# Ten gate tiles in pairs of seven half-block products, with the block sums kept in the place of the input's fp32 copy

## The chip, the cores and the metric

One core of a Trainium2 chip runs the whole layer as one program. The metric is the device time of one execution in microseconds (us); the kernel before has a median of 1524.26 us over three runs (1524.18 to 1525.2). Engines are named as in the profile: PE (TensorE matmul), PEld (its weight load), DVE (VectorE), ACT (ScalarE), POOL (GpSimd), SP (SyncE, which here only issues DMAs).

## The reference, cut to what matters

One layer: modulated attention of two branches (A windowed, B global), merged by sigmoid gates, then a ConvFFN. What this change touches is the modulated input `h`, the projection of the gates, and the query of branch B:

```
mod = silu(c) @ w_mod + b_mod                     # 6 vectors of 1024
h = x * (1 + scale1) + shift1                     # 1024 tokens x 1024
proj = h @ w_in + b_in                            # q_a, k_a, v_a, q_b, k_b, v_b, gates (2048 columns)
q_b = rope(qk_rms(proj[q_b columns]))
g_a, g_b = split(sigmoid(proj[gate columns]))     # 2 x 1024 channels
y = (g_a * (o_a @ w_branch_a) + g_b * (o_b @ w_branch_b)) @ w_out
```

The mod vectors `scale1` and `shift1` are needed before `h`; the other four and two for the context tokens are computed later, beside the projections.

## The kernel before, in words

All matmuls are in fp32 precision by parts: each operand is split into a high part `hi` (written as fp32r) and a low part `lo = x - hi`; `split` (L80) makes both, `mm3` (L89) issues hi·hi, hi·lo and lo·hi into one accumulation. So one 128x128 weight tile against 512 tokens is three matmul instructions, and each weight tile of 128x512 needs one split: `hi` on ACT (L82) and `lo` on DVE or POOL (L87).

**Stage 1 (L200 to L306).** `h` is kept transposed: eight tiles of 128 channels by 1024 tokens. For each of them SP loads x (`xr`, L218) and two tiles of `w_mod`, DVE computes shift and scale as dot products (`mod`, L193, one instruction of 128x1024), ACT writes `hh` (L241) and, in place, the fp32 `h` (L242), DVE writes `hl` (L245). PE meanwhile accumulates the eight token tiles of q_b in the eight banks of PSUM (L303 to L306). At its end DVE writes the eight q_b tiles to SBUF (`q_evac`, L378).

**The projections (L816 to L868).** An `order` list, built from `GORD` (L46, L805), interleaves 16 gate tiles with four groups: qa and qb (w_qa against four token tiles each) and ka and kb (w_kv against five each). A gate tile (`gate`, L769) is 128 channels by 1024 tokens: for each half of 512 tokens, eight channel tiles times three matmuls, 48 in all; then a sigmoid on ACT (L783) and a store to DRAM on ACT's queue (L784). With `GORD = 3, 4, 4, 1, 4` the order is 3 gates, qa, 4 gates, qb, 4 gates, ka, 1 gate, kb, 4 gates. Weights come through a ring of `RAWB` raw tiles (`fetch_raw`, L699) and are split ahead of their use (`prefetch`, L716) into a ring of eight split tiles (`wsplit`, L160). A gate's `lo` parts are on POOL (L722), those of the four groups on DVE.

Beside these, after each block of matmuls, run the remaining 48 mod vectors: `mods` (L755) spreads them by a span of PE time, each a 512 KB load by SP into a ring of `WRING` tiles (L751) and one DVE instruction. `side_step` (L794) takes one step at a time of the work on finished projections: rms and rotary of q_b (`qpost`, L383), rotary of q_a, and the keys (`kv_post`, L423).

**Order on the queues.** Up to the start of the ka group all five engines are under `manual_schedule` (L269, closed at L822): each engine executes its instructions in the order in which the program traces them, SP's DMAs too. After it a scheduler orders them. A waiting instruction holds up everything behind it on its engine.

**Memory.** `hp` is a pool of 19 slots of 128x1024 fp32 (L129), handed out and given back by name (`ht`, `hput`). In stage 1 the x tiles and `w_mod` tiles are temporary in it (`tmp`, L187).

## Time and profile before

| | us |
|---|---|
| median of three runs | 1524.26 |
| the profiled execution, its own time | 1523.1 |
| its span, first to last instruction | 1521.3 |
| PE busy in the span | 1503.2 (99%) |
| DVE / ACT / POOL busy in the span | 1168.3 / 786.1 / 751.3 |
| first and last matmul of a gate start at | 56.2 and 332.2 |

The profiled execution shows 1.8 us around its span, and it is 1.2 us below the median of the runs. A timeline row gives start, duration, engine, line, operation and tiles, and in brackets the idle time before it and what ended that. A row of windows gives the stretch, its length, and busy time (instructions) of PE, PEld, DVE, ACT and POOL, then the granted clock, the DMA share and GB/s. Times in the rows are from the start of the span.

### The profile page before, as it was taken

What the parts mean: (1) busy time and instruction counts of PE and PEld (TensorE: products, weight loads), DVE (VectorE), ACT (ScalarE), POOL (GpSimd) and SP (SyncE); (2) the same over time, 40 slices, a digit from 0 to 9 for tenths busy, and PEclk for the clock granted to TensorE, in tenths of its full rate; (3) what the DMA queues carried; (4) which work ended last, traced back from release to release, by engine and by line L of the source; (5) the groups of instructions that cost most, each with busy time, mean ns of one, the idle gap of its engine ahead of it and who ended that gap; (6) DMA issues with size and microseconds to landing.
All of it is one profiled execution on the core that took longest, in us unless ns stands there. A gap on an engine that the chain in (4) does not pass through costs nothing.

```text
span 1521.3 us, 22183 instructions
## 1 busy us (share of the span) xinstructions
PE 1503.2 (99%) x7812; PEld 1263.3 (83%) x7812; DVE 1168.3 (77%) x1751; ACT 786.1 (52%) x1303; POOL 751.3 (49%) x727
## 2 busy tenths in 40 slices
PE   8999999999999999999999999999999999999997
PEld 7888888888988888887888998888888888888887
DVE  6667986539988787877865788888888888557884
ACT  5322222439988677667234555444444444435552
POOL 0356532426776677766124346666666773111121
PEclk9999999999999999999999999999999999999998
DMA  9777672322234576653541322333344448996731
GB/s 370 266 242 242 223 252 87 106 82 68 67 108 104 131 172 167 153 121 89 207 160 42 104 77 98 111 111 111 111 111 111 112 111 238 340 271 210 255 105 56
DMA packets 114399, 232.09 MB, mean 153 GB/s; under 512 B 13200, under 2 KB 28048, under 8 KB 114192
## 3 DMA queue, kind: packets, MB, share of 16 engines
q1 hardware_dynamic: 99056, 201.82, 39.8%
q0 software_dynamic: 10400, 20.19, 8.8%
q10 hardware_dynamic: 4832, 8.68, 1.5%
q8 instruction: 61, 1.00, 0.3%
q14 instruction: 50, 0.41, 0.1%
HBM read 179.45 MB, written 65.86 MB: 161 GB/s over the span
## 4 chain that ended last, share of the span: by engine, by line
PE 92%; DVE 3%; ACT 2%; issue 1%; DMA 1%; POOL 1%; SPq 0%; DVEq 0%; ACTq 0%; POOLq 0%
PE ptr L604 5%; PE p L90 4%; PE p L91 4%; PE p L92 4%; PE g L90 4%; PE g L92 4%; PE g L91 4%; PE av L627 4%; PE av L628 3%; PE b L90 3%; PE b L92 3%; PE b L91 3%; PE s L496 3%; PE s L497 3%; PE c L90 2%; PE c L92 2%
## 5 line engine op out<-in xcount | busy, mean ns | idle before, releaser
L616 DVE TENSOR_TENSOR ptl<-ptr,pth 128x512 fp32r<-128x512 f32 x195 | 128.2, 685 | 20.2 <-ACT pth L615 18.0
L547 ACT ACTIVATE p<-p,nm 128x1280 f32<-128x1280 f32 (+2 forms) x128 | 139.8, 1093 | 6.6 <-DVE p L545 5.9
L87 DVE TENSOR_TENSOR ld<-rd,hd 128x1024 fp32r<-128x1024 f32 x77 | 94.8, 1250 | 50.5 <-ACT hd L82 48.3
L615 ACT CAST pth<-ptr 128x512 fp32r<-128x512 f32 x195 | 111.3, 590 | 30.3 <-PE ptr L604 28.7
L82 ACT CAST hd<-rd 128x1024 fp32r<-128x1024 f32 x77 | 79.3, 1048 | 82.2 <-PE p L92 55.7
L604 PEld LDWEIGHTS ptr<-identr,pb 128*128 128x128 f32 x944 | 96.3, 140 | 23.7 <-ACT pb L550 3.0
L604 PE MATMUL ptr<-identr,pb 128*128 128x128 f32 x944 | 107.5, 245 | 1.5 <-ACT pb L550 1.0
L87 POOL TENSOR_TENSOR wlg<-wg,whg 128x512 fp32r<-128x512 f32 x32 | 48.6, 1529 | 121.7 <-ACT whg L82 80.8
L627 PE MATMUL av<-pth,VT 128*128 128x512 f32 x236 | 104.2, 441 | 0.5 <-ACT side L639 0.3
L90 PE MATMUL p<-hd 128*128 128x512 f32 x264 | 103.2, 391 | 0.0
L92 PE MATMUL p<-hd,ld 128*128 128x512 f32 x264 | 102.8, 389 | 0.0
L91 PE MATMUL p<-ld,hd 128*128 128x512 f32 x264 | 102.7, 389 | 0.0
L90 PE MATMUL g<-hh,whg 128*128 128x512 f32 x256 | 99.9, 390 | 0.0
L92 PE MATMUL g<-hh,wlg 128*128 128x512 f32 x256 | 99.7, 389 | 0.0
L91 PE MATMUL g<-hl,whg 128*128 128x512 f32 x256 | 99.6, 389 | 0.0
L628 PE MATMUL av<-ptl,VT 128*128 128x512 f32 x236 | 97.5, 413 | 0.3 <-DVE ptl L616 0.2
L545 DVE TENSOR_SCALAR_CACHE_REDUCE p<-s,cvt,nmc 128x1024 f32<-128x1024 f32 x64 | 84.2, 1317 | 5.2 <-PE s L497 5.2
L496 PE MATMUL s<-KL,q 128*128 128x512 f32 (+2 forms) x192 | 73.6, 384 | 1.3 <-DVE p L545 0.8
L497 PE MATMUL s<-KL,q 128*128 128x512 f32 (+2 forms) x192 | 71.8, 374 | 0.0
L783 ACT ACTIVATE sg<-g,bgc 128x512 f32<-128x512 f32 x32 | 22.0, 686 | 96.2 <-PE g L92 91.4
L82 ACT CAST wS<-s 128x512 fp32r<-128x512 f32 x76 | 45.3, 620 | 48.7 <-POOL s L1236 47.9
L82 ACT CAST wA<-ru 128x512 fp32r<-128x512 f32 x57 | 35.5, 623 | 62.6 <-PE d L92 33.6
(434 smaller groups left out, 4866.9 us busy)
## 6 DMA issues: line engine op xcount, KB each, us to landing
wml<-in_wmodT_dram SPq DMA_DIRECT2D x48, 512.0 KB
ru<-in_w_up_dram SPq DMA_DIRECT2D x38, 512.0 KB
rd<-td SPq DMA_DIRECT2D x55, 256.0 KB
rd<-sd SPq DMA_DIRECT2D x44, 256.0 KB
rd<-in_w_dn_dram SPq DMA_DIRECT2D x33, 256.0 KB
wm<-in_wmodT_dram SPq DMA_DIRECT2D x16, 512.0 KB
wg<-in_w_g_dram SPq DMA_DIRECT2D x32, 256.0 KB
sgd<-sg ACTq DMA_DIRECT2D x32, 256.0 KB
```

The lines of the kernel that those rows point to most:

```text
L82: nc.scalar.copy(hi, src)
L87: lo_eng.tensor_tensor(out=lo, in0=src, in1=hi.bitcast(F32), op=ALU.subtract)
L90: nc.tensor.matmul(ps, a[0], b[0], start=start, stop=False, skip_group_check=resumed)
L91: nc.tensor.matmul(ps, a[0], b[1], start=False, stop=False, skip_group_check=resumed)
L92: nc.tensor.matmul(ps, a[1], b[0], start=False, stop=stop, skip_group_check=resumed)
L496: nc.tensor.matmul(o, self.q[0][:, hs], ks, start=True, stop=False)
L497: nc.tensor.matmul(o, self.q[1][:, hs], ks, start=False, stop=stop)
L547: nc.scalar.activation(row, row, AF.Exp, bias=self.nm[:, hs], scale=-1.0, accum_out=self.sm[:, hs])
L604: i = nc.tensor.transpose(tr[:, h * P:(h + 1) * P], self.bits[:, h, n * P:(n + 1) * P], identr)
L616: nc.vector.tensor_tensor(out=lo, in0=tr, in1=hi.bitcast(F32), op=ALU.subtract)
L627: nc.tensor.matmul(self.av, v, hi, start=first, stop=False)
L628: nc.tensor.matmul(self.av, v, lo, start=False, stop=self.left == 0)
```

## The change

Gates 2 to 11 are computed in five pairs. For a pair the weights are seen as 2x2 blocks A11, A12, A21, A22 (two gate tiles by two halves of the 1024 channels) and `h` as blocks B11, B12, B21, B22 (two halves of the channels by two halves of the tokens). The product of 2x2 blocks is formed from seven block products instead of eight (`spair`): A11·B11, S2·T2, S1·T1, S3·T3, A12·B21, S4·B22, A22·T4, with four sums of weight blocks S1 to S4 (`ssum`, POOL) and four sums of input blocks T1 to T4. A product is 4 channel tiles times 3 matmuls (`sprod`); the results are combined on DVE, ACT and POOL, and each of the four half tiles goes through the sigmoid and to DRAM (`gout`).

The input sums are made once (`hbuild`), in place of the fp32 copies `xr`, which now keep their slots through stage 1 instead of being temporary, and are split into tiles of their own. To have room, the q_b tiles go from PSUM through a small buffer to DRAM (`qd`) and are read back after the last pair; rope tables are loaded then too, and the q_b work (`qpost(1, t)`) is queued from there. The pool has 20 slots, the ring of mod weights 3 tiles instead of 4, the raw ring 4 instead of 3, the `pw` buffers 6 instead of 5, and the scratch of GpSimd's DMAs is 4096 instead of 8192. The order is now gates 0 and 1, the five pairs, qa, qb, ka, kb, gates 12 to 15. Every second `lo` of the qa and qb weights moves from DVE to POOL, and `side_step` always takes one new item.

```diff
-GORD = 3, 4, 4, 1, 4
-PWB = 5
+GORD = 0, 0, 0, 0, 4
+NPAIR = 5
+PWB = 6
...
-RAWB = 3
+RAWB = 4
...
-WRING = 4
+WRING = 3
...
+    qd = [dpool.tile([P, 2, HALF], F32, tag=f"qd{n}", name=f"qd{n}") for n in range(NT // 2)]
...
-    hfree = [(hp, f"H{n}") for n in range(19)]
+    hfree = [(hp, f"H{n}") for n in range(20)]
...
-    ropet = ht("ropet", (P, 2, NT, HD))
-    ropec, ropes = ropet[:, 0], ropet[:, 1]
...
-        x = tmp(f"xr{k}")
+        x = ht(f"xr{k}")
...
-        nc.sync.dma_start(ropec, rope_c)
-        nc.sync.dma_start(ropes, rope_s)
...
-    sqq = [ht("sqq", (P, 2, 512))]
...
-        q_evac(1, t, acc[t], bias_qb)
+        q = pw(f"qb{t}")
+        nc.vector.tensor_tensor(out=q, in0=acc[t], in1=bias_qb, op=ALU.add)
+        nc.sync.dma_start(qd[t // 2][:, t % 2], q)
+    hB = {}
+    def hbuild(k):
+        (b11, b12), (b21, b22) = [[st1[f][1][:, hf * HALF:(hf + 1) * HALF] for hf in (0, 1)] for f in (k, k + 4)]
+        def sub(e, o, a, b):
+            e.tensor_tensor(out=o, in0=a, in1=b, op=ALU.subtract)
+        def parts(n, src, e):
+            if k == 3 and n != "A22":
+                t = [qp.tile([P, HALF], R32, tag={"S1": "q1", "S2": "q2", "S3": "qs"}[n], name=f"T{n}{a}", bufs=2)
+                     for a in "hl"]
+            else:
+                t = ht(f"T{n}_{k}", (P, 2, HALF), R32)
+                t = [t[:, 0], t[:, 1]]
+            split(src, *t, nc.scalar, e)
+            hB[n, k] = t
+        sub(nc.vector, b11, b12, b11)
+        sub(nc.gpsimd, b12, b22, b12)
+        sub(nc.vector, b22, b22, b11)
+        parts("S1", b11, nc.vector)
+        sub(nc.gpsimd, b21, b21, b22)
+        parts("S2", b22, nc.vector)
+        parts("S3", b12, nc.gpsimd)
+        parts("A22", b21, nc.vector)
+        hput(f"xr{k}", f"xr{k + 4}")
...
+    sraw, sw = {}, {}
...
+            if gi == "s":
+                f = 2 * k + 2
+                sraw[k, f"A1{a + 1}"] = r = raw(f"ws{k}_{a}")
+                nc.sync.dma_start(r.rearrange("p (a b) -> p a b", b=P), w_g[f][:, 4 * a:4 * a + 4])
+                for b in (0, 1) if a == 0 else ():
+                    sraw[k, f"A2{b + 1}"] = r = pw(f"wt{k}_{b}")
+                    nc.sync.dma_start(r.rearrange("p (a b) -> p a b", b=P), w_g[f + 1][:, 4 * b:4 * b + 4])
+                continue
...
+        if gi == "s":
+            return
...
-        w, c = wsplit(wr, f"{nm}{k}"), None
+        w, c = wsplit(wr, f"{nm}{k}", "gpsimd" if gi > 1 and k % 2 else "vector"), None
...
-    wring, sring = ([hfree.pop(0) for _ in range(n)] for n in (WRING, 2))
...
-    queue = [qpost(1, t) for t in range(NT)]
-    gates = list(range(2 * KT))
+    queue = []
+    gates = [0, 1] + list(range(2 + 2 * NPAIR, 2 * KT))
+    def ssum(j, n):
+        def sub(o, a, b, op=ALU.subtract):
+            nc.gpsimd.tensor_tensor(out=o, in0=a, in1=b, op=op)
+        if n == "S1":
+            sraw[j, "S1"] = e = pw(f"we{j}")
+            sub(e, sraw[j, "A21"], sraw[j, "A22"], ALU.add)
+        elif n == "S3":
+            sraw[j, "S3"] = r = sraw.pop((j, "A21"))
+            sub(r, sraw[j, "A11"], r)
+        elif n == "S2":
+            sraw[j, "S2"] = r = sraw.pop((j, "A11"))
+            sub(r, sraw[j, "S1"], r)
+        else:
+            sraw[j, "S4"] = r = sraw.pop((j, "A12"))
+            sub(r, r, sraw.pop((j, "S2")))
+            raws[1] += 2
+    SLE = {"A11": "gpsimd", "S2": "vector", "S1": "gpsimd", "S3": "vector", "A12": "gpsimd", "S4": "vector",
+           "A22": "vector"}
+    def ssplit(j, n):
+        sw[j, n] = wsplit(sraw[j, n], f"s{n}_{j}", SLE[n])
+    HB = {"A11": (0, 0), "A12": (4, 0), "S4": (4, 1)}
+    def sprod(j, n, o, start):
+        h, l = sw.pop((j, n))
+        for k in range(4):
+            c = slice(k * P, (k + 1) * P)
+            if n in HB:
+                f, hf = HB[n]
+                b = [x[:, hf * HALF:(hf + 1) * HALF] for x in hT[k + f]]
+            else:
+                b = hB[n, k]
+            mm3(o, (h[:, c], l[:, c]), b, start and k == 0, k == 3, not start)
+        mods(12)
+    def sfirst(j):
+        ssum(j, "S1")
+        ssum(j, "S3")
+        ssplit(j, "A11")
+        ssum(j, "S2")
+        for n in ("S2", "S1", "S3"):
+            ssplit(j, n)
+    def gout(o, src, f, hf):
+        nc.scalar.activation(o, src, AF.Sigmoid, bias=bgc[:, f:f + 1])
+        nc.scalar.dma_start(sgd[f][:, hf * HALF:(hf + 1) * HALF], o)
+    def spair(j, more):
+        f = 2 * j + 2
+        a, b, c, d = (acc_tile(f"s{n}{j}") for n in "abcd")
+        pe, ve = (ph1.tile([P, 512], F32, tag="kv", name=f"{n}{j}", bufs=KVB) for n in ("pe", "ve"))
+        y = [p.tile([P, 2, HALF], F32, tag=t, name=f"y{n}_{j}", bufs=1) for n, (p, t) in enumerate(sring)]
+        y11, y12, y21, y22 = y[0][:, 0], y[0][:, 1], y[1][:, 0], y[1][:, 1]
+        def add(e, o, p, q):
+            e.tensor_tensor(out=o, in0=p, in1=q, op=ALU.add)
+        sprod(j, "A11", a, True)
+        nc.scalar.copy(pe, a)
+        ssplit(j, "A12")
+        sprod(j, "S2", b, True)
+        add(nc.vector, ve, b, pe)
+        ssum(j, "S4")
+        ssplit(j, "S4")
+        fetch_raw()
+        if more:
+            ssum(j + 1, "S1")
+            ssum(j + 1, "S3")
+        sprod(j, "S1", c, True)
+        nc.scalar.copy(y22, c)
+        ssplit(j, "A22")
+        sprod(j, "S3", d, True)
+        add(nc.vector, y22, d, y22)
+        add(nc.gpsimd, y22, y22, ve)
+        if more:
+            ssplit(j + 1, "A11")
+            ssum(j + 1, "S2")
+        else:
+            pf()
+        sprod(j, "A12", a, False)
+        gout(y11, a, f, 0)
+        gout(y22, y22, f + 1, 1)
+        if more:
+            ssplit(j + 1, "S2")
+        else:
+            pf()
+        sprod(j, "S4", c, False)
+        add(nc.vector, y12, c, ve)
+        if more:
+            ssplit(j + 1, "S1")
+        else:
+            pf()
+        gout(y12, y12, f, 1)
+        sprod(j, "A22", d, False)
+        add(nc.vector, y21, d, ve)
+        if more:
+            ssplit(j + 1, "S3")
+        else:
+            pf()
+        gout(y21, y21, f + 1, 0)
+        if not more:
+            hput(*[f"T{n}_{k}" for k in range(4) for n in ("S1", "S2", "S3", "A22") if k < 3 or n == "A22"])
...
-        n = 0 if slow[0] and turn[0] % 2 else 1
+        n = 1
...
-    order = []
+    order = [("g", gates.pop(0)) for _ in (0, 1)] + [("s", j) for j in range(NPAIR)]
...
-    rawq += [(gi, k, a) for gi, k in order for a in ((0, 1) if gi == "g" else (0,))]
+    rawq += [(gi, k, a) for gi, k in order for a in ((0, 1) if gi in ("g", "s") else (0,))]
...
-    for _ in range(WRING // 2):
-        fetch()
...
-    ahead = [2 if gi in (0, 2, 3) else 4 for gi, _ in order]
-    span[1] = sum(6 * KT if gi == "g" else 1.5 * len(groups[gi][2])
+    ahead = [2 if gi in (0, 2, 3) else 8 if gi == "s" else 4 for gi, _ in order]
+    span[1] = sum(6 * KT if gi == "g" else 84 if gi == "s" else 1.5 * len(groups[gi][2])
...
-    nxt = 0
+    nxt = [0]
+    def pf():
+        prefetch(*order[nxt[0]])
+        nxt[0] += 1
+    pf()
+    pf()
+    wring = [hfree.pop(0) for _ in (0, 1)]
+    for k in range(4):
+        hbuild(k)
+    wring.append(hfree.pop(0))
+    sring = [hfree.pop(0) for _ in (0, 1)]
+    for _ in range(2):
+        fetch()
...
-        while nxt < len(order) and sum(ahead[n:nxt + 1]) <= 8:
-            prefetch(*order[nxt])
-            nxt += 1
+        while nxt[0] < len(order) and sum(ahead[n:nxt[0] + 1]) <= 8:
+            pf()
+        if gi == "s":
+            spair(k, k + 1 < NPAIR)
+            if k + 1 == NPAIR:
+                ropet = ht("ropet", (P, 2, NT, HD))
+                ropec, ropes = ropet[:, 0], ropet[:, 1]
+                nc.sync.dma_start(ropec, rope_c)
+                nc.sync.dma_start(ropes, rope_s)
+                sqq = [ht("sqq", (P, 2, 512))]
+                for t in range(0, NT, 2):
+                    Q[1, t] = ht(f"Q1_{t}", (P, 2, 512))
+                    nc.sync.dma_start(Q[1, t], qd[t // 2])
+                queue += [qpost(1, t) for t in range(NT)]
+            continue
...
+                    if order[n + 1:n + 2] == [("s", 0)]:
+                        sfirst(0)
...
-    nc = _bacc.Bacc("TRN2", target_bir_lowering=False, num_devices=1, dynamic_dma_scratch_size=8192)
+    nc = _bacc.Bacc("TRN2", target_bir_lowering=False, num_devices=1, dynamic_dma_scratch_size=4096)
```

In the diff `sraw` holds raw weight tiles, `sw` their split parts, `sring` two slots for the four half tiles of a pair; `pe` and `ve` are intermediate sums, and `b11` to `b22` are the four halves of two `xr` tiles.

## The prediction

> **What bounds the kernel now.** I read the page first, then the projections by windows, then the engines' timelines around the first gate, where the change puts its new work.
>
> ```profile
> PE 1503.2 (99%) x7812; PEld 1263.3 (83%) x7812; DVE 1168.3 (77%) x1751; ACT 786.1 (52%) x1303; POOL 751.3 (49%) x727
> ```
> ```profile
> 56.20:90.00 33.80, 33.80 (x150) 27.97 (x149) 22.23 (x38) 9.36 (x14) 10.96 (x14) 1.00 0.73 251
> ...
> 110.00:155.00 45.00, 45.00 (x200) 37.29 (x199) 34.75 (x64) 12.07 (x19) 30.29 (x30) 1.00 0.75 254
> ...
> 175.00:220.00 45.00, 45.00 (x200) 37.28 (x199) 40.27 (x53) 10.84 (x18) 21.76 (x14) 1.00 0.71 250
> ...
> 326.00:345.00 19.00, 17.65 (x116) 15.02 (x114) 9.54 (x29) 12.51 (x33) 4.38 (x9) 1.00 0.22 70
> ```
>
> PE is busy for all of each stretch of projections, at a granted clock of 1.00. So a matmul removed here is worth its full cadence, and a wait of PE that is added here is paid in full: nothing later gives it back, since PE is 99% busy over the span. DVE is the second load: 40.27 of 45 us near 200 us, without holding PE.
>
> **The matmuls removed.** The pace of PE comes from two rows of one gate; between their starts lie 22 steps of three matmuls.
>
> ```profile
> 62.12 0.39 PE L92 MATMUL g<-hh,wlg 128*128 128x512 f32 x1
> ...
> 77.08 0.39 PE L92 MATMUL g<-hh,wlg 128*128 128x512 f32 x1
> ```
>
> 14.96 us for 66 matmuls is 0.2267 us each (the 0.39 us of a row overlaps its neighbours). Ten gates had 10 x 48 = 480; five pairs have 5 x 7 x 12 = 420. 60 x 0.2267 = **13.6 us less** PE work. A gate is 10.9 us, a block product 2.72 us, a pair 19.04 us.
>
> **The start of gate 0.** Today gate 0 starts straight behind the q_b matmuls, because its weights were loaded and split beforehand:
>
> ```profile
> L90 PE MATMUL g<-hh,whg x256: 387/389/466, 56.2 to 331.8; 128*128 128x512 f32 x128
> ```
> ```profile
> 37.11 4.92 SPq L705 DMA_DIRECT2D wg<-in_w_g_dram  x3
> ```
> ```profile
> 49.52 1.65 ACT L82 CAST whg<-wg 128x512 fp32r<-128x512 f32 x3
> ```
> ```profile
> 50.20 3.79 POOL L87 TENSOR_TENSOR wlg<-wg,whg 128x512 fp32r<-128x512 f32 x3 [38.80 <-DMA gcol<-in_qg_dram]
> ```
> ```profile
> 51.67 5.45 DVE L378 TENSOR_TENSOR Q<-q1acc,bias_qb 128x512 f32<-128x512 f32 x8 [1.74 <-PE q1acc L92]
> ```
>
> The change traces eight stores of q_b on SP ahead of `fetch_raw`. SP is under the manual order, so the loads of gate 0, issued at 37 us today, now stand behind a store that waits for the last of the eight DVE evacuations, at 51.67 + 5.45 = 57.1 us. How long a load takes to land I bound by a wait for one:
>
> ```profile
> 127.18 1.33 SPq L751 DMA_DIRECT2D wml<-in_wmodT_dram  x3
> ```
> ```profile
> 131.39 1.28 DVE L193 CUSTOM_DVE_ANT_0 wml<-wml,sc,bmc 128x1024 f32<-128x1024 f32 x1 [1.59 <-DMA wml<-in_wmodT_dram]
> ```
>
> That is at most 4.2 us from the first of three issues (0.44 us each) for 512 KB; the gate's tile is 256 KB, so I take 3.0, with 2 and 4.2 as ends. [...] Then: issue 57.5, landed 60.5, `hi` 0.55 us on ACT to 61.1, `lo` 1.26 us on POOL to 62.4, where the third matmul can go; today that one starts at 56.2 + 0.45 = 56.7. **+5.7 us** (4.7 to 7), and the two gates end at 56.2 + 21.8 + 5.7 = 83.7.
>
> **The input sums and the first pair.** `hbuild` is traced after the splits of gates 0 and 1 and before everything else of the projections, so on POOL and DVE all of it goes ahead of the first pair's weights and of the mod vectors. For each of four k it has three operations on POOL and five on DVE, all with both inputs in SBUF. Alone they cost 1.26 us (POOL, 3.79 / 3) and 0.61 us (DVE, two in the 1.21 us before the next start). The mod vector is 1.20 us, start to start:
>
> ```profile
> 60.42 1.27 DVE L193 CUSTOM_DVE_ANT_0 wml<-wml,sc,bmc 128x1024 f32<-128x1024 f32 x1
> 61.62 0.07 DVE L193 DVE_READ_ACCUMULATOR2_ANT modc<- 128x1 f32 x1
> 61.62 1.27 DVE L193 CUSTOM_DVE_ANT_0 wml<-wml,sc,bmc 128x1024 f32<-128x1024 f32 x1
> ...
> 145.81 1.28 DVE L87 TENSOR_TENSOR wlqb<-wqb,whqb 128x512 fp32r<-128x512 f32 x2
> 147.02 1.27 DVE L193 CUSTOM_DVE_ANT_0 wml<-wml,sc,bmc 128x1024 f32<-128x1024 f32 x1
> ```
>
> But POOL and DVE don't run such operations side by side:
>
> ```profile
> 57.03 2.23 DVE L193 CUSTOM_DVE_ANT_0 wml<-wml,sc,bmc 128x1024 f32<-128x1024 f32 x1
> ...
> 175.53 2.47 DVE L376 SCALAR_TENSOR_TENSOR Q<-accqb,bias_qa 128x512 f32<-128x512 f32 x4
> ...
> 181.81 1.75 DVE L193 CUSTOM_DVE_ANT_0 wml<-wml,scc,bmc 128x1024 f32<-128x1024 f32 x1
> ...
> 183.49 2.30 DVE L193 CUSTOM_DVE_ANT_0 wml<-wml,scc,bmc 128x1024 f32<-128x1024 f32 x1
> ```
> ```profile
> 56.90 1.29 POOL L87 TENSOR_TENSOR wlg<-wg,whg 128x512 fp32r<-128x512 f32 x1 [2.91 <-ACT whg L82]
> ...
> 176.58 1.30 POOL L87 TENSOR_TENSOR wlg<-wg,whg 128x512 fp32r<-128x512 f32 x1 [1.12 <-ACT whg L82]
> ...
> 182.56 2.16 POOL L340 TENSOR_TENSOR Q<-rt1q,rt2q 128x512 f32<-128x512 f32 x1
> ```
>
> POOL runs from 56.90 to 58.19, and the mod vector that starts at 57.03 takes 2.23 us instead of 1.27: the rest of POOL's operation longer. At 182.56 POOL starts inside a mod vector and takes 2.16, and the mod vector after it 2.30. They take turns. The four evacuations from PSUM at 175.53 don't show this: 0.62 us each beside POOL. So the sum of both engines counts, except where DVE reads PSUM.
>
> Per k the operations also depend on each other in a line (b12 on POOL, b22 on DVE, b21 on POOL, then splits), so I take the plain sum, 3 x 1.26 + 5 x 0.61 = 6.8 us. POOL: four gate splits 61.1 to 66.1, four k to 93.4, less 0.6 for the first `b11`, done early: 92.8. Then two weight sums and the `lo` of A11, taking turns with two of DVE's mod vectors: 3 x 1.26 + 2 x 1.20 = 6.2, to 99.0. A11 could have had its third matmul at 84.2. Meanwhile DVE has, ahead of the `lo` of S2, five mod vectors (72 units of span at 672 / 48 = 14 each), the small operations of `prepare` (1.2 us, 59.20 to 60.42 today) and five turns of POOL: 6.0 + 1.2 + 0.6 + 5 x 1.26 = 14.1, to 106.9, where the product S2 needs it at 83.7 + 2.7 + 0.5 = 86.9. **+20.0 us** of PE waiting, in two pieces. If the two engines ran side by side, POOL alone would set it: 66.1 + 12 x 1.26 = 81.2, and the waits would come to about 3 us; that is the lower end, 22 the upper.
>
> **The pairs.** DVE has per pair six mod vectors, four `lo` and four sums from PSUM; POOL four weight sums, three `lo` and one output sum. With both inputs in SBUF that is 7.2 + 2.4 + 8 x 1.26 = 19.7 us of turns against PE's 19.04. With the four PSUM sums in line too (0.68 us each) it is 22.4. The up stage works in the same seven products, and there is PE's pace kept:
>
> ```profile
> 940.00:1100.00 160.00, 160.00 (x708) 132.50 (x707) 139.58 (x126) 78.33 (x110) 108.43 (x60) 1.00 0.32 109
> ```
>
> DVE and POOL are at 87% and 68% there, waits for each other included. The pairs lack its order by a scheduler: POOL must do its output sum, which waits for DVE's `y22` behind that product's mod vectors, before the `lo` of the next pair's A11. I take 21.0, between 19.7 and 22.4: 2.0 us too long for the 4.7 pairs behind the first S2, **+9.4 us** (3 to 16; 0 if the up stage is the model).
>
> [...]
>
> **What costs nothing.** ACT gains seven splits and two copies per pair, some 9 us of 19; it has 12.07 of 45 us now. The ring of three mod tiles makes SP wait for the mod vector before last but one: SP has nothing else due then, as raw tiles come a pair ahead; if DVE is late SP is late with it, which is in the turns above. The stores and reloads of q_b (2 MB each way) lie in a stretch at DMA share 0.73; PE doesn't wait for them except through SP at the start. The q_b work moves behind the pairs, into qa, qb and ka. No gates lie between the groups any more; the last four gates, 43.5 us, still follow kb. PE idles 19.00 - 17.65 = 1.35 us at that end now; I add **1 us** (-1 to 4) for work that is left over. The halved scratch may delay POOL's DMAs in attention; nothing in the rows shows its limit, and I count it within the same bound.
>
> **Sum.** -13.6 + 5.7 + 20.0 + 9.4 + 1.0 = +22.5 us on the profiled execution's 1523.1: 1545.6. The median of the runs is 1.2 above it: **1547 us**. A difference under 0.2%, 3 us, would count as none.
>
> **Rivals.** *Side by side* (ends faster): POOL's and DVE's operations overlap in `hbuild`, which ends by 81 us, and the pairs keep PE's pace. Then -13.6 + 5.7 + 3 = -4.9: 1519 us. For it: PE was held by nothing while DVE stood at 40 of 45. Against: the rows that take turns. It decides at 13.6 us of waits in all. Chance 0.09; with 10 us of waits more or less between it and the forecast, no difference has 0.03.
>
> *Pairs at PE's pace*: the start as forecast, the pairs like the up stage: -13.6 + 5.7 + 20.0 + 1 = +13.1, 1537 us. Against it, 19.7 is over 19.04. Chance 0.25, with short waits at the first pair included down to 1528.
>
> *Pairs in a line*: all of DVE and POOL in turn, 22.4 us and more, if a late DVE also holds SP's loads: +16 to +20 in place of 9.4, 1554 to 1558. Chance 0.13.
>
> The forecast itself has 0.50. Slower in all 0.88. The range 1528 to 1557 leaves out the side-by-side case, the no-difference case and the end of the last one, and takes in the ends of the loads' landing and of the first pair's waits.
>
> **What would show it.** In the changed profile: the first gate matmul near 61 us and its loads on SP after 57; about 27 us of DVE and POOL alternating behind it, with 1.26 us operations of POOL at 1.8 or more; two gaps of PE near 84 to 107, released by POOL's `lo` of A11 and DVE's `lo` of S2; pairs of about 21 us, with PE waiting at A11 of each. Wrong if gate 0 starts before 58, if the gaps at the first pair are together under 10 us, or if pairs take 19.1.

## The result, and the profile after

The change makes the kernel slower: 1573.39 us median (1571.09 to 1574.65, four runs) against 1524.47 for the kernel before on the same chip, ratio 1.0318 (95% interval 1.0301 to 1.0336). The forecast was 1547, its range ended at 1557. The sign was right and the size was missed by 26 us. The profiled execution took 1571.09 us with a span of 1569.3, 48.0 more than the 1521.3 of before.

The page of the kernel after: busy time, then PE and its granted clock in 40 slices of 39 us.

```profile
PE 1510.4 (96%) x7752; PEld 1259.3 (80%) x7752; DVE 1220.6 (78%) x1803; ACT 809.6 (52%) x1344; POOL 818.5 (52%) x767
...
PE   9869989799999999999999999999999999999997
...
PEclk9989999899999999999999999999999999999999
```

The 60 matmuls are gone (7752 instead of 7812), and PE is "busy" longer all the same: some matmuls take longer (up to 0.79 us instead of 0.39, in the rows below), as at 61.8 us, with a granted clock of 0.50 from 61 to 65 us. All digits under 9 but the last lie in the first eight slices, the projections. The windows of the kernel after, cut where its stages change (first pair, qa, qb, ka, kb, last gates); the columns are those of the windows of before:

```profile
56.00:96.00 40.00, 24.67 (x98) 19.26 (x96) 24.52 (x28) 15.32 (x25) 26.51 (x18) 0.85 0.52 171
96.00:212.00 116.00, 105.45 (x422) 81.57 (x422) 84.31 (x114) 38.93 (x66) 61.38 (x39) 0.95 0.70 233
212.00:240.00 28.00, 23.93 (x98) 19.14 (x97) 15.24 (x23) 8.76 (x16) 12.73 (x16) 0.94 0.90 315
240.00:262.00 22.00, 22.00 (x98) 18.22 (x98) 20.85 (x35) 8.42 (x15) 19.58 (x18) 1.00 0.57 193
262.00:289.00 27.00, 26.77 (x118) 21.84 (x118) 27.00 (x43) 5.49 (x9) 26.48 (x30) 1.00 0.36 107
289.00:331.00 42.00, 32.47 (x128) 25.21 (x127) 41.82 (x117) 11.12 (x28) 17.67 (x18) 0.84 0.27 79
331.00:379.00 48.00, 46.84 (x226) 38.46 (x225) 27.49 (x74) 14.58 (x42) 18.61 (x25) 1.00 0.29 94
```

Before, PE filled every such window from 56 to 331 us at a granted clock of 1.00 (from 96 to 212 us, 116.00 of 116 us). Now it does so only beside qb. DVE is full from 262 to 331 us. The waits of PE between 56 and 380 us (sum, times, longest) say at which operand:

```profile
PE sa L91 <- ACT whsA L83: 10.3, 1, 10.3
PE g L91 <- ACT whg L83: 5.5, 1, 5.5
PE sd L91 <- DVE y L885: 5.0, 4, 2.2
PE acckb L92 <- DVE wlkb L88: 4.2, 1, 4.2
PE sb L93 <- DVE wlsS L88: 4.2, 1, 4.2
PE acckb L91 <- DVE kv L1027: 4.1, 1, 4.1
PE accqa L91 <- ACT whqa L83: 3.9, 1, 3.9
```

The first, second and fifth are the first pair and the start, as forecast. The third is in the pairs, but not at the place named; the seventh and kb's two were not forecast. The start itself looks as it was drawn, the stores of q_b on SP, the loads behind them, and ACT's split at 61.1 us:

```profile
52.25 5.08 SPq L413 DMA_DIRECT2D qd<-qb  x8
57.42 1.85 SPq L741 DMA_DIRECT2D wg<-in_w_g_dram  x4
```
```profile
61.12 1.29 ACT L83 CAST whg<-wg 128x512 fp32r<-128x512 f32 x2 [11.55 <-DMA wg<-in_w_g_dram]
```

The rows of the tiles give the places (instruction, count, shortest/median/longest in ns, first and last start):

```profile
L93 PE MATMUL g<-hh,wlg x96: 387/389/792, 63.1 to 378.3; 128*128 128x512 f32 x96
...
L93 PE MATMUL sb<-TS,wlsS x15: 392/398/632, 106.6 to 195.1; 128*128 128x512 f32 x15
...
L91 PE MATMUL accqa<-whqa,hh x32: 389/389/628, 211.8 to 238.9; 128*128 128x512 f32 x32
...
L91 PE MATMUL acckb<-whkb,hh x24: 387/389/628, 289.1 to 327.0; 128*128 128x512 f32 x24
...
L93 PE MATMUL acckb<-whkb,cl x16: 389/389/628, 302.5 to 330.5; 128*128 128x512 f32 x16
```

The 48 us come apart as follows: the third and fourth line against PE's own work at 0.2267 us a matmul, the others against the same stage of before.

| place | us | forecast |
|---|---|---|
| matmuls removed | -13.6 | -13.6 |
| gate 0: its third matmul at 63.1 instead of 56.7 | +6.4 | +5.7 |
| from there to S2's third matmul, at 106.6: 43.5 for 108 matmuls (24.5) | +19.0 | +20.0 |
| from there to qa, at 211.8: 105.2 for 406 matmuls (92.0) | +13.2 | +9.4 |
| qa +6.1, qb -0.1, ka +0.5, kb +11.8 | +18.3 | } +1.0 |
| last gates +2.7, behind them +1.9 | +4.6 | } |

The terms for gate 0 and for the first pair are right, and that for the pairs is 3.8 us too small. The term for what is left over, 1 us, measured 23.

Of the +13.2, 5.4 us are waits of PE, 5.0 of them the third line of that list. Some 1.7 us each are lost in two stretches in which the granted clock is about 0.50 (107.6 to 111.0 and 165.6 to 169.0 us), and 2.5 us are left in small pieces. The other 1.9 us are PE's own pace: matmuls that read a tile of input sums start 0.234 us apart, the others 0.227. An undisturbed product of such a tile takes 2.81 us instead of 2.72, and a pair 19.43 instead of 19.04. Where e7 (below) puts halves of the input's own tiles in the place of the sums, those products take 2.72 too. So the seven products save 11.7 us here, not 13.6.

### The profile page after: what moved, and what is told of

Same layout as the page of the kernel before. It is cut to its first block, busy times and chain, and to the rows that moved or that the text cites. A ratio compares the mean times of both kernels' runs of the same rounds, so it can differ in the third digit from the quotient of the medians.

```text
span 1569.3 us, 22261 instructions
## 1 busy us (share of the span) xinstructions
PE 1510.4 (96%) x7752; PEld 1259.3 (80%) x7752; DVE 1220.6 (78%) x1803; ACT 809.6 (52%) x1344; POOL 818.5 (52%) x767
## 4 chain that ended last, share of the span: by engine, by line
PE 79%; DVE 8%; DMA 3%; POOL 3%; ACT 3%; issue 3%; SPq 0%; ACTq 0%; DVEq 0%; POOLq 0%
PE ptr L631 5%; PE p L91 4%; PE p L92 4%; PE p L93 4%; PE av L654 4%; PE av L655 3%; PE b L91 3%; PE b L93 3%; PE b L92 3%; PE s L523 3%; PE s L524 3%; PE c L91 2%; PE d L93 2%; PE c L93 2%; PE c L92 2%
## 5 line engine op out<-in xcount | busy, mean ns | idle before, releaser
L643 DVE TENSOR_TENSOR ptl<-ptr,pth 128x512 fp32r<-128x512 f32 x195 | 128.1, 684 | 19.7 <-ACT pth L642 17.5
L88 DVE TENSOR_TENSOR wS<-s,wS 128x512 fp32r<-128x512 f32 x57 | 56.9, 1023 | 4.9 <-ACT wS L83 4.9
L193 DVE CUSTOM_DVE_ANT_0 wml<-wml,sc,bmc 128x1024 f32<-128x1024 f32 x32 | 53.7, 1695 | 8.7 <-DMA wml<-in_wmodT_dram 8.7
L91 PE MATMUL a<-B,wA 128*128 128x512 f32 x152 | 59.1, 389 | 0.0
L92 PE MATMUL a<-B,wA 128*128 128x512 f32 x152 | 59.1, 389 | 0.0
L93 PE MATMUL a<-B,wA 128*128 128x512 f32 x152 | 59.1, 389 | 0.0
```

Of the source, the lines that this page charges most:

```text
L88: lo_eng.tensor_tensor(out=lo, in0=src, in1=hi.bitcast(F32), op=ALU.subtract)
L91: nc.tensor.matmul(ps, a[0], b[0], start=start, stop=False, skip_group_check=resumed)
L92: nc.tensor.matmul(ps, a[0], b[1], start=False, stop=False, skip_group_check=resumed)
L93: nc.tensor.matmul(ps, a[1], b[0], start=False, stop=stop, skip_group_check=resumed)
L643: nc.vector.tensor_tensor(out=lo, in0=tr, in1=hi.bitcast(F32), op=ALU.subtract)
```

## The experiments

Each changes the kernel after, and was timed against the kernel before on the same chip, where that took 1523.9 to 1524.7 us. "Excess" is the median less that of the kernel before; the kernel after has 48.9.

| run | median us | ratio (95%) | excess | less than after |
|---|---|---|---|---|
| e1 loads first | 1563.74 | 1.0258 (1.0243, 1.0273) | 39.6 | 9.3 |
| e2 no weight sums | 1553.19 | 1.0192 (1.0177, 1.0207) | 29.1 | 19.8 |
| e3 reloads spread | 1566.42 | 1.0278 (1.0261, 1.0295) | 42.3 | 6.6 |
| e4 no q_b work | 1558.80 | 1.0232 (1.0208, 1.0256) | 34.7 | 14.2 |
| e5 gates between | 1566.46 | 1.0273 (1.0256, 1.0290) | 41.8 | 7.1 |
| e6 no mod loads | 1573.64 | 1.0319 (1.0303, 1.0334) | 49.0 | -0.1 |
| e7 no input sums | 1556.43 | 1.0203 (1.0188, 1.0218) | 31.8 | 17.1 |
| e8 = e1 + e3 + e5 | 1554.96 | 1.0196 (1.0178, 1.0214) | 30.3 | 18.6 |
| e9 y22 first | 1571.38 | 1.0309 (1.0292, 1.0326) | 47.4 | 1.5 |
| e10 half of q_b late | 1568.69 | 1.0292 (1.0277, 1.0308) | 44.8 | 4.1 |
| e11 = e1 + e3 + e9 + e10 | 1554.67 | 1.0201 (1.0186, 1.0216) | 30.7 | 18.2 |
| e12 = e11, vectors first | 1546.73 | 1.0139 (1.0122, 1.0156) | 22.1 | 26.8 |
| e13 = e12, two k at a time | 1549.12 | 1.0167 (1.0150, 1.0184) | 24.7 | 24.2 |
| e14 = e12, four gates first | 1540.69 | 1.0106 (1.0090, 1.0122) | 16.3 | 32.6 |

**The start (e1).**

```diff
+    for f_ in (0, 1):
+        for a_ in (0, 1):
+            early["g", f_, a_] = wr_ = raw(f"wg{f_}_{a_}"), None
+            nc.sync.dma_start(wr_[0].rearrange("p (a b) -> p a b", b=P), w_g[f_][:, 4 * a_:4 * a_ + 4])
     for t in range(NT):
         q = pw(f"qb{t}")
```

> The only edit: SP's loads of gates 0 and 1 are traced ahead of the eight q_b stores. My theory: gate 0 starts near 56.2 us instead of 61.8, and since POOL's first splits and with them the whole line of input sums begin earlier, the third matmul of A11 and of S2 come about 6 us earlier as well; PE's work and waits behind that are unchanged, so the time falls by about 6 (4 to 9) us, to some 1567. Rival: the input sums have their own start (the last of the q_b evacuations on DVE), so that gate 0 gains 5.6 us but the first pair's weights come no earlier, PE waits as much longer there, and the time stays within 2 us of 1573.

Gate 0 started at 56.3 us, and A11's and S2's third matmuls came at 90.3 and 98.7 instead of 98.2 and 106.6. So the late loads cost 8 to 9 us (7.9 at these matmuls, 9.3 in the medians), not only the 5.5 of gate 0: POOL's line of input sums stands behind the splits of those loads and passes its delay on.

**The input sums (e7).** The sums and their splits are left out.

```diff
-        sub(nc.vector, b11, b12, b11)
...
-        parts("A22", b21, nc.vector)
+        for n, hf in (("S1", 0), ("S2", 1), ("S3", 1), ("A22", 0)):
+            hB[n, k] = [x[:, hf * HALF:(hf + 1) * HALF] for x in hT[k]]
```

> Leaves out the input sums and their splits (eight operations for each of four k): the products take halves of the input's own split tiles in their place, so gates 2 to 11 are not the reference's. Loads, weight sums, mod vectors and matmuls stay. My theory: the two waits at the first pair, 18.6 us in all by the third matmul of S2 (at 106.6 us where PE could have been at 88), are these operations on POOL and DVE; without them it comes at 87 to 90, and the time falls by 17 to 20 us, to 1553 to 1556. Rival: the first pair's weights are late in any case, since eight mod vectors and the weight sums stand ahead of them and their loads follow the q_b stores: S2 comes at 95 or later and the time falls by 11 us or less.

The two waits at the first pair are gone from the list of waits, S2's third matmul came at 89.5 us, and everything behind it stayed as it was (105.8 us to qa, 41.4 for kb). The input sums cost 17 us in this place. The rival, that the first pair is late anyway, falls.

**The pairs (e2, e6, e9).** In e2 each sum of weight blocks is left out and a raw block stands for it.

```diff
-            sub(e, sraw[j, "A21"], sraw[j, "A22"], ALU.add)
+            sraw[j, "S1"] = sraw[j, "A22"]
...
-            sub(r, sraw[j, "A11"], r)
+            sraw[j, "S3"] = sraw.pop((j, "A21"))
```

> Leaves out the four sums of weight blocks S1 to S4 in each pair: a raw block stands in the place of each, so the gate columns are not the reference's. Matmuls, splits, mod vectors and all loads stay. My theory: DVE and POOL take turns in operations with both inputs in SBUF, and the turns bound the pairs. Four sums of 1.26 us fewer take them from 19.7 to 14.7 us a pair, under PE's 19.04, so pairs fall from about 22.2 to 19.1 us: 4.7 pairs, about -13 us, to some 1558 to 1562. Rival: the pairs are held by the loads (mod tiles in a ring of three, raw weights a pair ahead), and stay at 22 us; the time stays within 3 us of 1573.

From S2's third matmul to qa 94.0 us instead of 105.2. The wait at qa went too (21.8 instead of 27.8 us), and S2's third matmul came 2.0 us earlier. That gives more than I had expected, and it fits two readings: four turns fewer, or one hand-off fewer, as DVE's low parts of S2, S3 and S4 wait for a high part on ACT, and that for a sum on POOL.

In e6 the loads of the mod vectors 4 to 36 are left out; the vectors are computed from the first three tiles.

```diff
+            if n < WRING or n >= 36:
+                w = pool.tile([P, T], F32, tag=tag, name=f"wml{n}", bufs=1)
                 nc.sync.dma_start(w, wmodT[late[n][0]])
+            else:
+                w = fetched[n - WRING]
```

> Leaves out the loads of the mod weights of the vectors 4 to 36, which are computed from the three tiles loaded first, so their values are not the reference's. All instructions of the engines stay. Theory A, the turns: DVE and POOL alternate and DVE reaches the sum for y22 late, so that the seventh product waits; the loads don't matter, and the pairs stay at 105 us from the first S2 to qa (103 to 106), the time within 4 us of 1573 but for up to 6 us in qa, whose weights wait for the reloads. Theory B, the queue on SP: raw weights wait for POOL's last sum, the mod tiles stand behind them on SP, and DVE waits up to 3 us for a mod tile ahead of the sum for y22; without the loads the pairs take 96 to 100 us and the time falls by 6 to 10 us or more.

No change (-0.1 us, and 106.2 us from S2 to qa). Theory B, the queue on SP, falls, although DVE waits 9.6 us for these tiles in the pairs of the kernel after. The same wait of PE is there without them:

```profile
PE sd L91 <- DVE y L888: 5.2, 3, 2.2
```

In e9 the sum that the seventh product waits for is traced ahead of S3's mod vectors.

```diff
-        mods(12)
+        if n != "S3":
+            mods(12)
...
         add(nc.vector, y22, d, y22)
         add(nc.gpsimd, y22, y22, ve)
+        mods(12)
```

> The reference's result; the only edit is one of order on DVE in the pairs: the sum that frees the bank of the seventh product (y22, of the bank of S3 with the copy of S1) is traced ahead of S3's mod vectors instead of behind them. The seventh product waited for that sum in four of the five pairs, 0.8, 2.4, 1.3 and 1.1 us over the cadence, with slower matmuls behind each wait. Theory A, a place in line: DVE has time enough in a pair and only this sum stands behind too much; then the waits go, nothing takes their place, the pairs from the first S2 to qa take 96 to 99 us instead of 105.2, and the time falls by 6 to 9 us. Theory B, the sum of the turns: what DVE and POOL do in a pair is longer than PE's work, so that another product waits as long (the low parts of A11 or S2 late); the pairs stay at 103 us or more and the time within 3 us of 1573.

1.5 us, with intervals that overlap, and 103.3 us from S2 to qa. In its list of waits of the pairs the one named is down from 5.0 to 1.9 us, and two others have grown from 0.4 and nothing:

```profile
PE sd L91 <- DVE y L886: 1.9, 2, 1.0
PE sa L93 <- POOL wlsA L88: 1.6, 4, 0.9
PE sb L91 <- ACT whsS L83: 0.5, 1, 0.5
```

So it isn't that one sum's place in line (theory A as I had put it). But theory B says more than this shows. The lists of waits of DVE, ACT and POOL in the pairs of the kernel after, 105 us, one line of each:

```profile
DVE wlsS L88 <- ACT whsS L83: 21.6, 11, 3.2
```
```profile
ACT whsS L83 <- POOL ws L829: 21.7, 7, 3.6
```
```profile
POOL wlsA L88 <- ACT whsA L83: 22.8, 4, 5.7
```

DVE stands a fifth of the time for ACT, ACT as long for POOL, and POOL for ACT. All three execute in the order of the trace, and DVE has mod vectors ready behind the instruction that waits (at 129.68 us it has stood 1.27 us for ACT, and the two vectors behind it, from 130.29 us, wait for nothing).

**Hand-offs or turns (e12).** On top of e11 (below), the mod vectors of three more products are traced ahead of the split that DVE waits in.

```diff
-        mods(12)
+        if n not in ("S1", "S3", "S4") and (n != "A11" or j == 0):
+            mods(12)
...
         add(nc.vector, ve, b, pe)
+        mods(12)
         ssum(j, "S4")
         ssplit(j, "S4")
...
+        mods(12)
         if more:
             ssplit(j + 1, "S2")
...
+            mods(12)
             ssplit(j + 1, "S3")
```

> The reference's result: the four edits of the run before it together, and in the pairs the mod vectors of three more products are traced ahead of the split that DVE waits in (S4, and S2 and S3 of the next pair). Order on DVE, and of the loads on SP behind it, is all that changes. DVE stood 21.6 us of the pairs in line for a high part on ACT, which stood as long for a weight sum on POOL, with mod vectors ready behind. Theory A, hand-offs in line: DVE does the vectors in that time, fewer of them meet POOL's work later, and the pairs from the first S2 to qa fall from 103.1 to 95 to 99 us; the time from 1554.7 to 1547 to 1551. Theory B, the sum of the turns: in whatever order, DVE and POOL need as long for a pair; the pairs stay at 102 us or more and the time at 1553 to 1557.

From S2 to qa 96.9 us instead of 103.1, 1546.73 instead of 1554.67. No instruction was removed; SP's loads of the mod tiles move along, and e6 had shown that these don't hold the pairs. Three windows of its pairs, and PE's waits from 97 to 200 us, whose only line is the end of the first pair's:

```profile
107.00:130.00 23.00, 23.00 (x101) 18.71 (x100) 19.12 (x26) 9.20 (x16) 13.86 (x8) 1.00 0.89 287
130.00:153.00 23.00, 23.00 (x102) 18.74 (x101) 18.27 (x24) 8.60 (x15) 16.69 (x10) 1.00 0.82 266
153.00:176.00 23.00, 23.00 (x101) 18.70 (x100) 20.54 (x27) 8.38 (x14) 16.74 (x10) 1.00 0.77 247
```
```profile
PE sb L93 <- DVE wlsS L88: 3.8, 1, 3.8
```

PE fills the pairs. From the first matmul of the second pair to that of the fifth are 58.28 us, 19.43 for each, which is PE's own pace:

```profile
117.36 0.39 PE L91 MATMUL sa<-hh,whsA 128*128 128x512 f32 x1
...
175.64 0.39 PE L91 MATMUL sa<-hh,whsA 128*128 128x512 f32 x1
```

So hand-offs held them, theory A of this run is right, and the turns leave room. In the 69 us of the windows stand 22 mod vectors, 14 low parts on DVE and 27 operations of POOL: 22 x 1.20 + 14 x 0.61 + 27 x 1.26 = 69.0 us (by the durations of before). But by the starts and ends of their rows neither engine is in such an operation for 5.2 of the 69 us, so that sum counts a turn some 8% too dear. In one such moment POOL is done at 136.84 us and DVE stands until 137.53:

```profile
134.69 2.15 POOL L834 TENSOR_TENSOR ws<-we,ws 128x512 f32<-128x512 f32 x1
...
137.53 0.69 DVE L88 TENSOR_TENSOR wlsS<-ws,whsS 128x512 fp32r<-128x512 f32 x1 [1.82 <-ACT whsS L83]
```

The kernel after has 20, 13 and 23 of them in the same 69 us, 60.9 us by that sum, and neither engine is in one for 11.5 us. The groups of both kernels in that stretch, of e12 first, show what shared turns cost: 1.65 and 1.70 us in the mean for a mod vector that takes 1.27 alone (at 60.42 us of before).

```profile
L193 DVE CUSTOM_DVE_ANT_0 wml<-wml,sc,bmc 128x1024 f32<-128x1024 f32 x22 | 36.1, 1653 | 3.2 <-DMA wml<-in_wmodT_dram 3.2
```
```profile
L193 DVE CUSTOM_DVE_ANT_0 wml<-wml,sc,bmc 128x1024 f32<-128x1024 f32 x20 | 33.8, 1703 | 7.3 <-DMA wml<-in_wmodT_dram 7.3
```

**The reloads (e3).**

```diff
-                    nc.sync.dma_start(Q[1, t], qd[t // 2])
+                    if t == 0:
+                        nc.sync.dma_start(Q[1, t], qd[t // 2])
...
+        if gi == 2 and k in (1, 3, 5):
+            nc.sync.dma_start(Q[1, k + 1], qd[(k + 1) // 2])
```

> The only edit: the four reloads of q_b from memory go one at a time into the qa group (before its first, second, fourth and sixth tile) instead of all four behind the last pair and ahead of the loads of the qa weights. My theory: qa takes 27.8 us instead of 21.8 since its weights land late behind 2 MB of reloads and the rope tables; spread, qa takes 22 to 24 us, and the time falls by 4 to 6 us, to some 1568. Rival: what holds qa is ACT or DVE with the last pair's outputs; qa stays at 27 to 28 us and the time within 2 us of 1573.

qa took 21.8 us. SP's timeline, of the kernel after and of e3, shows the reloads and the next weights behind them:

```profile
213.18 5.13 SPq L993 DMA_DIRECT2D Q<-qd  x4
218.41 4.05 SPq L746 DMA_DIRECT2D wqa<-in_w_qa_dram  x4
```
```profile
213.27 0.40 SPq L994 DMA_DIRECT2D Q<-qd  x1
213.77 5.62 SPq L746 DMA_DIRECT2D wqa<-in_w_qa_dram  x4
```

The weights are issued 4.6 us earlier, and the wait is gone with all the matmuls that ran slowly behind it (0.43 us apart from 228.1 to 230.2 us, at a granted clock of 0.50). The reloads cost this only because SP came to them late, 1.4 us behind qa's first matmul. In e2 they stand ahead of the weights too, but SP issued them 2.9 us before that matmul (195.71 and 198.63 us), and qa took 21.8 us as well.

**The q_b work (e4, e5, e10).** In e4 its squares, scale and rotary are left out.

```diff
-                queue += [qpost(1, t) for t in range(NT)]
...
```

> Leaves out the work on the finished q_b tiles (squares, rms, scale and rotary), which the change moved behind the pairs; a constant stands for the scale. My theory: DVE is full from 250 to 330 us with that work, and kb waits for it (41.8 us instead of 27.2); without it kb takes 27 to 30 us and the time falls by 12 to 18 us, to 1556 to 1561. Rival: kb waits for its PSUM banks and the two buffers behind them because no gates lie between ka and kb any more, whatever work is left; kb stays at 38 us or more and the time falls by less than 5 us.

kb took 29.2 us instead of 41.4, the last gates 45.5 instead of 47.8; ka took 3.0 more. Without that work PE fills kb:

```profile
290.00:320.00 30.00, 30.00 (x148) 24.90 (x147) 26.48 (x97) 13.03 (x37) 14.65 (x16) 1.00 0.34 105
```

So DVE's load is the cause, and the lack of gates between the groups is not one by itself. What place has to do with it, e5 and e10 ask.

```diff
-GORD = 0, 0, 0, 0, 4
+GORD = 0, 1, 0, 1, 2
```

```diff
-                queue += [qpost(1, t) for t in range(NT)]
+                queue += [qpost(1, t) for t in range(4)]
...
+            if gi == 1:
+                queue += [qpost(1, t) for t in range(4, NT)]
```

> The only edit: one of the last four gates is traced ahead of qb and one ahead of kb; the work is the same. My theory: what kb waited for was DVE, full with the q_b work that the change had moved behind the pairs (leaving that work out made kb 12.2 us shorter); a gate costs DVE no weights, so 21.8 us of PE work ahead of kb let it catch up. kb and its gates then take PE's pace, less about 3 us for the cover that the end now lacks: the time falls by 7 to 12 us, to 1561 to 1566. Rival: DVE has as much work in all and is only late elsewhere; what kb gains, PE loses behind kb, where two gates are left to cover the keys, and the time stays within 3 us of 1573.

> The reference's result; the only edit: the work on the last four q_b tiles is queued behind kb's tiles instead of ahead of everything, so that it falls to the last gates, where DVE is busy 27.5 us of 48. My theory: kb waits for DVE's queue; half the q_b work less ahead of it gives half of what leaving it out gave, so kb takes 33 to 37 us instead of 41.4, and the last gates hide at least half of the moved work: the time falls by 3 to 7 us. Rival: the work appears as a wait behind the last gate, and the time stays within 2 us of 1573 or grows.

Both give a part: 7.1 and 4.1 us. But in e5 it doesn't come from where I expected it. From qa to the end of kb the kernel after takes 118.7 us and e5 141.8, of which the two gates are 21.8: 1.3 us more, with PE waiting 2.0 us at qb, 1.8 in ka and 5.5 in kb for DVE or POOL. The gain is 4.2 us in the last gates, which run at PE's pace when only two stand there (21.8 us), 2.5 in the pairs and 2.2 ahead of S2's third matmul (at 104.4 us); the same mod vectors are spread over more work there, which may be why. In e10 kb fell to 33.4 and ka rose from 27.7 to 36.4: DVE's queue came to the evacuation of qb's banks late, which ka needs.

```profile
PE accka L91 <- DVE Q L374: 6.3, 1, 6.3
```

The half that went behind kb was hidden there: the last gates took 45.5 us instead of 47.8. But the rotary of q_a moved up into its place, ahead of that evacuation (at 260.85 us; in the kernel after at 271.88, behind it). So in both runs a group still waits for DVE or POOL.

**Together (e8, e11).**

> The reference's result, with three edits in the order alone: loads of gates 0 and 1 ahead of the q_b stores, the q_b reloads spread over qa, one gate ahead of qb and one ahead of kb. If the three causes are separate their gains add up: 9.6 and 7.0 us measured for the first two and 7 to 12 for the third, so 1545 to 1550, still 20 to 25 us slower than the kernel before. Rival: they are one backlog of DVE and POOL seen at three places; the gains don't add up and the time is 1555 or more.

> The reference's result, with four edits of order together: loads of gates 0 and 1 ahead of the q_b stores, the sum y22 ahead of S3's mod vectors, the q_b reloads spread over qa, and half of the q_b work behind kb; the last four gates stay at the end. If each removes its own wait: 9.6 and 7.0 measured, 6 to 9 and 3 to 7 expected for the other two, so 1541 to 1548. It would still be 17 to 24 us slower than the kernel before, which is what the input sums (17 us when left out) and the rest of the pairs cost. Rival: waits move on to the next place, and the time is 1553 or more.

e8 gains 18.6 us where its parts gave 23.0, e11 18.2 where they gave 21.5. The start and the reloads add up, as separate causes would: in e8, S2's third matmul comes 7.8 us earlier than in e5, and qa is 5.4 us shorter. The rest is lost behind the last gate, where e8 took 4.2 us more than the kernel after, and again at ka, 37.6 us in e11.

**The input sums again (e13, e14).** e13 traces them for two k at a time, step by step; e14 moves two of the last four gates to the front and traces one k's sums ahead of each of the four gates there.

```diff
-    for k in range(4):
-        hbuild(k)
+    hbuild((0, 1))
+    hbuild((2, 3))
```

```diff
-GORD = 0, 0, 0, 0, 4
+GORD = 0, 0, 0, 0, 2
...
-    order = [("g", gates.pop(0)) for _ in (0, 1)] + [("s", j) for j in range(NPAIR)]
+    order = [("g", gates.pop(0)) for _ in range(4)] + [("s", j) for j in range(NPAIR)]
...
+    hbuild(0)
...
+        if n in (1, 2, 3):
+            hbuild(n)
```

> The reference's result: the five edits of order of the run before, and the input sums traced two k at a time, step by step, so that POOL and DVE always have an operation of the other k ready and neither stands for the other's result. The operations are the same. Theory A, the turns: the two engines exclude each other here, the sum of their durations is 27 us in any order, and the third matmul of S2 stays at 96.5 to 99.5 us (98.7 before); the time within 2 us of 1546.7. Theory B, the line of dependences, as it was in the pairs: the sums finish 5 us or more earlier, S2 comes at 94 us or before, and the time falls by 4 us or more.

> The reference's result: the five edits of order of the run before, and two of the last four gates moved to the front, with the input sums of one k traced behind each of the first three gates, ahead of any mod vector. My theory: the input sums cost only because nothing else stood for PE to do; 21.8 us more of gates cover them, S2's third matmul comes at 103 to 106 us where PE could have it at 103, so 14 to 17 us of waits go; at the end two gates are left to cover the work on the keys and on q_b, which gives 2 to 10 us back. 1533 to 1543. Rival: what DVE and POOL have to do up to the last gate is the bound wherever it is put, and the end gives back 14 us or more: 1546 or above.

In e13 DVE's last operation of the sums ended at 83.5 us, in e12 at 84.9: 26.6 and 27.9 us from the first. The plain sum is 12 x 1.26 + 20 x 0.61 = 27.3. In e13 one engine or the other is in such an operation for the whole 26.6 us. So here the turns are the limit in both orders, as the prediction had it. The edit also put the ring of mod tiles into slots that come free later, and the first pair's loads, behind those tiles on SP, were issued at 83.3 us instead of 78.7. POOL stood 9.3 us ahead of its first weight sum, and the run's excess is 2.6 us larger than e12's.

In e14 S2's third matmul came at 103.4 us, where PE alone puts it (57.1 + 204 x 0.2267 = 103.3): the 17.5 us of waits that e12 has there are gone. Only 5.8 us of them are left in the end. The pairs took 3.7 us more (the same mod vectors beside less PE work), qa 4.7, ka 2.0, and the part behind the last gate 5.4, while kb and the last gates took 3.3 and 1.6 less; ka waited for DVE as in e10:

```profile
PE accka L91 <- DVE Q L374: 7.7, 1, 7.7
```

The rival of that run is half right, as far as this shows: what DVE and POOL have to do before attention is too much for the PE work that is left there, so cover at one place is taken from another. e14 is the best version tried, 1.06% slower than the kernel before; none beats it.

## Why the prediction was wrong

- **Start**: right in mechanism and size (first gate matmul at 61.8, forecast 61.1). That the delay goes on through POOL's line to the first pair is in the next term, which starts that line at 61.1; so e1 wins back 8 to 9 us and not 5.7.
- **Input sums**: right. POOL ended them at 92.3 us (forecast 92.8), A11's and S2's third matmuls came at 98.2 and 106.6 (99.0 and 106.9). e7 prices them at 17 us, e13 shows turns as their limit. *Side by side* is refuted by this.
- **Pairs**: +13.2 instead of +9.4, within its bounds, but by another mechanism. The sum of turns, 19.7 us a pair, was taken for a floor and is none: in e12 the same operations fit into pairs of 19.43 us. PE's own 19.04 was 0.39 us too low, as its matmuls that read a tile of input sums start 0.234 us apart instead of 0.227. What I added for order (to 21.0) was put at another place: PE waited at the seventh product, for DVE's `y22`, and not at A11. Hand-offs between in-order engines took it; e12 takes 6 us of it back by order alone. *Pairs in a line* had a larger price, 16 to 20, for another reason. *Pairs at PE's pace* fits three pairs of e12, but not those of the kernel after.
- **The step that failed**: "What costs nothing", with "I add 1 us (-1 to 4) for work that is left over". It measured 23. Two costs stood in it as if they were none. I had written that PE doesn't wait for stores and reloads "except through SP at the start"; the reloads stood on SP ahead of qa's weights as the stores did ahead of gate 0's: 6 us. And "the q_b work moves behind the pairs, into qa, qb and ka" was costed at nothing without naming what hides it: 12 us in kb, 2.7 in the last gates; left out in e4, it gives 14.2 us. The row that spoke against it was quoted, DVE 40.27 of 45 us near 200 us, beside the four gates between qb and ka: DVE had little room even there, and those gates, which cost it no weights, had gone from between the groups.

Open is how much of qa to kb is turns of DVE and POOL and how much hand-offs; with the q_b work left out ka still waited 3.2 us for DVE, and no order of that stretch was tried as e12 tried it in the pairs.

## What to carry to other kernels

An edit that frees memory by moving work moves a load onto an engine: add up that engine's time in the stage that receives it before calling it free, and look at every queue that the moved transfers stand in, at both ends of the move. Where engines that hand over to each other execute in order, put the independent work ahead of the instruction that waits; here that alone took 6 of the 11 us that e11 still lost in the pairs. Fewer matmuls pay only as long as the sums that replace them find room beside PE, here 60 matmuls (13.6 us, 1.9 of them lost again to a slower pace) against 17 us of input sums.

## What the runs showed of the hardware

Some waits of PE cost more than their length here. The seventh product of the third pair, in the timeline of the kernel after:

```profile
164.88 0.48 PE L91 MATMUL sd<-TA,whsA 128*128 128x512 f32 x1 [2.19 <-DVE y L885]
...
167.42 0.63 PE L92 MATMUL sd<-TA,whsA 128*128 128x512 f32 x1
167.84 0.63 PE L93 MATMUL sd<-TA,wlsA 128*128 128x512 f32 x1
168.27 0.63 PE L91 MATMUL sd<-TA,whsA 128*128 128x512 f32 x1
168.70 0.53 PE L92 MATMUL sd<-TA,whsA 128*128 128x512 f32 x1
169.07 0.39 PE L93 MATMUL sd<-TA,wlsA 128*128 128x512 f32 x1
```

From 165.7 to 168.7 us seven matmuls come 0.43 us apart instead of 0.23 behind a wait of 2.19 us, some 1.6 us on top of it. The granted clock is 0.50 from 165.6 to 169.0 us, 0.95 in the mean of that stage, and 0.84 in kb. Behind the wait of 1.18 us in the next pair none did, and in e7 waits of 2.19 and 2.09 us slowed seven or eight and one of 2.03 us none. No run here shows what decides it.

e13's input sums agree with turns of DVE and POOL: an operation of POOL takes up to 1.71 us there and 1.26 alone, and one engine or the other is in an operation on them for all of the 26.6 us, 27.3 by the durations alone. As a budget those durations are a little too high: in e12's pairs they give 69.0 us where the rows cover 63.8.

Matmuls of the same shape ran at two paces: 0.234 us apart where the moving tile is one of the input sums, 0.227 where it is part of `hh` or `hl`. With `hh` and `hl` in the place of the sums, in e7, it is 0.227 there too. No run here shows why.
